# One level of Strassen's scheme in the up-projection of a gated MLP

## The chip, the cores and the metric

The kernel runs on one core of a Trainium2 chip, in one launch. The metric is device time in microseconds of that core; several runs give a median.

## The reference, cut to what matters

One hybrid decoder layer is computed in float32 for a prompt of 2048 tokens and for 8 single-token samples: a first mixing stage (causal pooling and differential attention), cross-attention into 256 memory tokens, and a gated MLP with a causal convolution of width 3 between its two projections. The change touches the MLP:

```python
D_MODEL, D_FF, CONV_W = 1024, 2816, 3

def conv_ffn(h, prefix, w_up, conv_w, conv_b, w_down):
    T = h.shape[1]
    up = h @ w_up                      # (T, 1024) @ (1024, 5632)
    upp = jnp.concatenate([prefix.astype(up.dtype), up], axis=1)
    c = conv_b
    for j in range(CONV_W):
        c = c + upp[:, j:j + T] * conv_w[j]
    a, g = c[..., :D_FF], c[..., D_FF:]
    return (jax.nn.silu(g) * a) @ w_down, upp[:, -(CONV_W - 1):]
```

## The kernel before

**Precision.** Every float32 operand of a large product is split into a rounded high part and a low part, both in the matmul format fp32r (`split`: ScalarE writes the high part, VectorE the difference). A product is three matmuls: low weight by high input, high by high, high weight by low input.

**Layout.** Activations lie transposed, features on the 128 partitions and tokens along the row, in four chunks `c` of 512 tokens; the last also has the 8 samples, `W = [512, 512, 512, 520]`. Its matmuls go in two pieces of 260 columns.

**Buffers.** Pool `hp` (function `H`) has 43 buffers of 4 KB a partition for weights, activations and intermediate tiles. Pool `rp` (opened by `raw_open` after the attention) has two more for raw weights, `sp` (`St`) six small ones. PSUM has two tiles of two banks (`PA`) and four of one bank (`PB`).

**Order of work.** The program is a list of items. An item names the weights that it needs, a function that issues its instructions, and a cost; `weave` mixes two lists by these costs, and `drive` (line 396) walks the list. Ahead of an item it stages coming weights in three steps (`Weight.stage`): the transfer on SyncE's queue, the high part on ScalarE, the low part on VectorE. `look(4, 3, 2)` says how many weights ahead each step is. `later` puts work off by some microseconds of cost, `due` calls it. The tile framework then orders the instructions of each engine and adds the waits; each engine and each queue takes its instructions in that order.

**The MLP.** `ffn_items(c)` (line 1649) goes through the 22 blocks `j` of 128 hidden features, in groups of two. For a block `ffn_up` (line 1471) projects the block of `a` (s = 0) and that of the gate (s = 1). Each is one weight of 1024 x 128 and 24 matmuls of 512 columns (`proj`, lines 429 and 432), a tile `up` in PSUM. ScalarE copies the tile to `Uf` (line 1477) and starts the convolution in `cc` (line 1478), VectorE adds two taps (lines 1484, 1485); the gate, the product and the split into `act` come later. After a group of two blocks `ffn_down` (line 1507) multiplies their `act` with two weights of 128 x 1024: for each of 8 output tiles, 6 matmuls into one PSUM bank (line 1524), and VectorE adds the tile to the residual `xf` (line 1531, for pieces of 260 line 1529).

**Around it.** `norm_steps` scales the input of the MLP and splits it into `h3hi` and `h3lo`, the operands `X[c]` (lines 261 to 267). The cross-attention of the samples (`sc_items` for queries and scores, `sc_items2` for values and output) is woven into chunk 0 of the MLP, norms and the final norm of the neighbouring chunks into chunks 1 to 3. Ahead of the MLP stand the input projections (`p1_items`), the pooling, the attention (`att_items`) and the cross-attention of the prompt.

## Time and profile before

| | us |
|---|---|
| median of 3 runs | 3143.33 (3138.91 to 3145.14) |
| the profiled execution, its own time | 3144.37 |
| its span | 3142.6 |
| TensorE matmuls busy | 3016.3 (96%) |
| TensorE weight loads busy | 2609.5 (83%) |
| VectorE busy | 2023.8 (64%) |
| ScalarE busy | 1369.2 (44%) |
| GpSimd busy | 439.5 (14%) |

The mean granted TensorE clock is 0.983 of full speed. Busy times overlap; a matmul's busy time runs on while the next has started, so the pace of a row of matmuls is read from one start to the next or from the chain of waits, not from the mean duration of one. The chain that ended last lies on TensorE for 60% of the span, up-projection 31% and down-projection 14%.

### The profile page before, as it was taken

What the parts mean: (1) busy time and instruction counts of PE and PEld (TensorE: products, weight loads), DVE (VectorE), ACT (ScalarE), POOL (GpSimd) and SP (SyncE); (2) the same over time, 40 slices, a digit from 0 to 9 for tenths busy, and PEclk for the clock granted to TensorE, in tenths of its full rate; (3) what the DMA queues carried; (4) which work ended last, traced back from release to release, by engine and by line L of the source; (5) the groups of instructions that cost most, each with busy time, mean ns of one, the idle gap of its engine ahead of it and who ended that gap; (6) DMA issues with size and microseconds to landing.
All of it is one profiled execution on the core that took longest, in us unless ns stands there. A gap on an engine that the chain in (4) does not pass through costs nothing.

```text
span 3142.6 us, 45471 instructions
## 1 busy us (share of the span) xinstructions
PE 3016.3 (96%) x17694; PEld 2609.5 (83%) x17694; DVE 2023.8 (64%) x3280; ACT 1369.2 (44%) x2187; POOL 439.5 (14%) x873
## 2 busy tenths in 40 slices
PE   7999999898999989999899999999999999999998
PEld 6889899787897886799777777888888878899998
DVE  5725654568677686645578777766766666766566
ACT  5524444456655423333344444434444433443342
POOL 0134234211111153300000000000000100000000
PEclk9999999999999999999999999999999999999999
DMA  8556356543533385463465334342333433243321
GB/s 285 180 160 218 101 169 187 147 131 120 157 100 109 141 268 195 140 215 132 159 236 180 127 122 151 120 154 91 94 104 118 162 95 112 88 142 96 94 81 71
DMA packets 378203, 451.98 MB, mean 144 GB/s; under 512 B 18321, under 2 KB 292248, under 8 KB 377972
## 3 DMA queue, kind: packets, MB, share of 16 engines
q1 hardware_dynamic: 336925, 349.29, 34.7%
q0 software_dynamic: 27264, 89.03, 8.2%
q10 hardware_dynamic: 13798, 10.76, 1.1%
q8 instruction: 139, 2.28, 0.3%
q14 instruction: 77, 0.62, 0.1%
HBM read 364.57 MB, written 84.85 MB: 143 GB/s over the span
## 4 chain that ended last, share of the span: by engine, by line
PE 60%; DVE 4%; DMA 2%; issue 1%; ACT 1%; POOL 1%; SPq 0%; DVEq 0%; ACTq 0%; POOLq 0%
PE up L429 21%; PE down L1524 14%; PE up L432 10%; PE wo L443 4%; PE vo L94 2%; PE vo L95 2%; PE vo L96 2%; PE S L94 1%; PE S L96 1%; PE S L95 1%; DMA vg<-in_cache_v_dram,idx 1%; DVE wlo L297 1%; DMA mixr<-mix_d 1%; PE O L1123 1%; POOL vg L951 1%
## 5 line engine op out<-in xcount | busy, mean ns | idle before, releaser
L429 PE MATMUL up<-h3hi,wlo 128*128 128x512 f32 (+1 forms) x1760 | 562.6, 352 | 7.5 <-DVE wlo L297 6.8
L429 PE MATMUL up<-h3hi,whi 128*128 128x512 f32 (+1 forms) x1760 | 560.2, 351 | 0.0
L297 DVE TENSOR_TENSOR wlo<-wraw,whi 128x1024 fp32r<-128x1024 f32 x432 | 520.4, 1219 | 50.3 <-ACT whi L294 49.6
L294 ACT CAST whi<-wraw 128x1024 fp32r<-128x1024 f32 x432 | 443.2, 1047 | 195.0 <-DMA wraw<-in_w_down_dram 95.9
L1524 PE MATMUL down<-act,whi 128*128 128x512 f32 (+1 forms) x1760 | 447.5, 352 | 10.9 <-DVE xf L1531 10.1
L432 PE MATMUL up<-h3lo,whi 128*128 128x512 f32 (+1 forms) x1760 | 357.7, 349 | 0.0
L429 PEld LDWEIGHTS up<-h3hi,wlo 128*128 128x128 f32 x1760 | 308.6, 189 | 56.8 <-ACT whi L294 3.8
L429 PEld LDWEIGHTS up<-h3hi,whi 128*128 128x128 f32 x1760 | 308.8, 189 | 46.4
L1524 PEld LDWEIGHTS down<-act,whi 128*128 128x128 f32 x1760 | 293.8, 188 | 60.4 <-DVE xf L1531 13.8
L1484 DVE SCALAR_TENSOR_TENSOR cc<-Uf,vec,cc 128x512 f32<-128x512 f32 x176 | 132.0, 750 | 328.5 <-ACT cc L1478 324.0
L1477 ACT COPY Uf<-up 128x512 f32<-128x512 f32 (+1 forms) x176 | 103.3, 587 | 509.9 <-PE up L432 507.0
L432 PEld LDWEIGHTS up<-h3lo,whi 128*128 128x128 f32 x1760 | 285.6, 188 | 46.6
L1524 PE MATMUL down<-act,wlo 128*128 128x512 f32 (+1 forms) x880 | 279.4, 350 | 0.4 <-DVE wlo L297 0.4
L1483 POOL COPY halo<-Uf 128x2 f32<-128x2 f32 x176 | 44.2, 251 | 1388.0 <-ACT Uf L1477 1377.4
L1531 DVE TENSOR_TENSOR xf<-xf,down 128x512 f32<-128x512 f32 (+1 forms) x308 | 205.5, 682 | 44.7 <-PE down L1524 41.1
L1089 ACT ACTIVATE T<-T,mn 128x1024 f32<-128x1024 f32 (+4 forms) x192 | 171.9, 897 | 132.1 <-DVE mn L1082 122.3
L1071 PE MATMUL sc<-K,Q 128*128 128x512 f32 (+5 forms) x640 | 171.2, 385 | 18.7 <-DVE mn L1082 18.4
L1082 DVE CUSTOM_DVE_ANT_0 T<-sc,Dt 128x1024 f32<-128x1024 f32 (+7 forms) x128 | 125.8, 985 | 76.2 <-PE sc L1071 74.5
L1524 PEld LDWEIGHTS down<-act,wlo 128*128 128x128 f32 x880 | 154.0, 188 | 24.8 <-DVE wlo L297 1.2
L443 PE MATMUL z<-h1hi,wlo 128*128 128x512 f32 (+1 forms) x480 | 158.4, 363 | 4.8 <-DVE pps L668 4.4
L443 PE MATMUL z<-h1hi,whi 128*128 128x512 f32 (+1 forms) x480 | 153.9, 353 | 0.0
L1123 PE MATMUL O<-V,wT 128*128 128x128 f32 x1088 | 149.2, 278 | 1.8 <-ACT wT L1114 1.3
(417 smaller groups left out, 5846.5 us busy)
## 6 DMA issues: line engine op xcount, KB each, us to landing
wraw<-in_w_up_dram SPq DMA_DIRECT2D x176, 512.0 KB
wraw<-in_w_down_dram SPq DMA_DIRECT2D x88, 512.0 KB
wraw<-in_w_in_dram SPq DMA_DIRECT2D x32, 512.0 KB
Q<-q_d SPq DMA_DIRECT2D x64, 256.0 KB
wraw<-in_w_out_dram SPq DMA_DIRECT2D x32, 512.0 KB
wraw<-m_d SPq DMA_DIRECT2D x32, 512.0 KB
wraw<-vo_d SPq DMA_DIRECT2D x32, 512.0 KB
K<-k_d SPq DMA_DIRECT2D x24, 512.0 KB
```

The costliest lines, as they stand in the source:

```text
L294: S.copy(self.hi[:, :1024], self.raw[:, :1024])
L297: V.tensor_tensor(self.lo[:, :1024], self.raw[:, :1024], f(self.hi[:, :1024]), ALU.subtract)
L429: PE.matmul(out, w[wi][:, kt, :], kslice(hi, kt, c0, n), start=kt == 0 and wi == 1, stop=False)
L432: PE.matmul(out, w[0][:, kt, :], kslice(lo, kt, c0, n), start=False, stop=kt == KT - 1)
L443: PE.matmul(out, w[wi][:, kt, :], kslice(z, kt, c0, n), start=i == 0, stop=i == 3 * KT - 1)
L1071: PE.matmul(ps[:, j * 512:j * 512 + w], v3(Q[c], 2)[:, z, self.t * P:(self.t + 1) * P], K[c][hf][:, c0:c0 + w], start=z == 0, stop=z == 1)
L1082: V.tensor_tensor_reduce(out, pin, din, -SLOPE[self.h], 3.0e38 if hf == 0 else mn[:, 0:1], ALU.add, ALU.min, mn[:, hf:hf + 1])
L1089: S.activation(tg[:, :mg], tg[:, :mg], AF.Exp, bias=mn[:, last:last + 1], scale=-1.0, accum_out=self.l[:, 2 * g + c:2 * g + c + 1])
L1123: PE.matmul(O[:, self.t * P:(self.t + 1) * P], self.wt[g][:, (j % 4) * P:(j % 4 + 1) * P], v3(Vt[j // 8], 8)[:, j % 8, :], start=j == 0, s ...
L1484: V.scalar_tensor_tensor(cc[:, :CH], U[:, 1:1 + CH], vc(CWT + FT + nt), cc[:, :CH], ALU.mult, ALU.add)
L1524: PE.matmul(out, ws[p][wi][:, nt, :], act[:, z + c0:z + c0 + n], start=st_ and p == 0, stop=en and p == 1)
L1531: V.tensor_tensor(sv(xx, c), sv(xx, c), view, ALU.add)
```

## The change

One level of Strassen's scheme (in the form with 15 additions) is put on the up-projection. For a block `j` the pair of weights, `a` and gate, is taken as a matrix of 2 x 2 parts: the two halves of the 1024 input features by the two outputs. The chunk's tokens are two halves of 256 (260 in the last chunk). Seven products (`p1`, `p6`, `p5`, `p3`, `p2`, `p7`, `p4` in `ffn_up`) of 512 features by 128 outputs by 256 tokens take the place of eight; each is 12 matmuls.

- Four of the seven weights are sums of parts. `sums_items` makes them once per block, in high and low parts, and writes them to a DRAM tensor `s_d`; blocks 0 to 7 beside the projections of the first two chunks, 8 to 21 beside those of the last two and the attention. In the MLP they are read back as they are (`Stored`, tile `shl`). The other three are half-size weights, split as before (`HalfWeight`, tile `whl`, raw data in four buffers of `rp`).
- The seven token operands of a chunk are made by `xop_items`, in high and low parts, from the scaled input, which is no longer split by `norm_steps`.
- VectorE adds the products out of PSUM, seven additions a pair; ScalarE only copies the first. The conv's first step reads the sum in SBUF.
- The down-projection takes groups of four blocks (`GROUPS`, the last has two), so that a PSUM tile sums 12 matmuls of four blocks; its weights come as 512 rows x 256 columns, and its tiles are spread between the products of the next group.
- `NBUF_H` goes from 43 to 41. `look(6, 3, 2)` is set for the MLP. `sc_items2` moves to chunk 1.

The diff, cut:

```diff
+GROUPS = [4] * 5 + [2]
+HW = CX // 2
-NBUF_H = 43
+NBUF_H = 41
+    qp = ctx.enter_context(tc.tile_pool(name="qp", bufs=6))
+    s_d = [dr.tile([P, 2, 2, 2, 512], F32, name=f"s_d{j}") for j in range(NF)]
...
+    class HalfWeight:
+        def stage(self, n):
+            if n == 0:
+                self.raw = rp[0].tile([P, 512], F32, tag="raw", name="wraw2")
+                SY.dma_start(v3(self.raw, 4, P), self.src)
+            elif n == 1:
+                self.hl = H("whl", F32R)
+                S.copy(self.hl[:, :512], self.raw)
+            else:
+                V.tensor_tensor(self.hl[:, 512:1024], self.raw, f(self.hl[:, :512]), ALU.subtract)
...
+    class Stored(HalfWeight):
+        def stage(self, n):
+            if n == 0:
+                self.hl = H("shl", F32R)
+                SY.dma_start(f(v3(self.hl, 2)), self.src)
...
+        def add(j):
+            def fn(_):
+                wa, wg = st[j]
+                a1, a2, g1, g2 = wa[:, :512], wa[:, 512:1024], wg[:, :512], wg[:, 512:1024]
+                V.tensor_tensor(g2, g1, g2, ALU.add)
+                V.tensor_tensor(g1, a1, g1, ALU.subtract)
+                V.tensor_tensor(a1, g2, a1, ALU.subtract)
+                V.tensor_tensor(a2, a2, a1, ALU.subtract)
+            return item([], fn, 0, 2.5)
+        def part(j):
+            def fn(_):
+                for i, t in enumerate(st.pop(j)):
+                    hi, lo = H("shi", F32R), H("slo", F32R)
+                    split(hi[:, :1024], lo[:, :1024], t[:, :1024])
+                    for z, p in enumerate((hi, lo)):
+                        ST.dma_start(s_d[j][:, i, z].rearrange("p s n -> p (s n)"), f(p[:, :1024]))
...
+        def parts(key, src):
+            hi, lo = H("xhi", F32R), H("xlo", F32R)
+            for i in range(2):
+                split(k4(hi)[:, 2 * i:2 * i + 2, :n], k4(lo)[:, 2 * i:2 * i + 2, :n], src[i])
+            out[key] = k4(hi)[:, :, :n], k4(lo)[:, :, :n]
...
+        return [item([], fn, 0, 2.5) for fn in (p1, t1, t2, q2, t3, p2, t4)]
-    def ffn_up(c, j, s):
-            _, view = proj(c, X[c], ws[0], "up")
-            S.copy(sv(U[:, 2:2 + w], c), view)
-            S.activation(sv(cc[:, :w], c), view, AF.Identity, bias=vc(CB + nt), scale=vc(CWT + 2 * FT + nt))
+    def ffn_up(c, j):
+        def product(out, ws, key):
+            (wh, wl), (xh, xl) = ws[0], X[c][key]
+            for k in range(4):
+                for wi in (wl, wh):
+                    PE.matmul(out, wi[:, k, :], xh[:, k], start=k == 0 and wi is wl, stop=False)
+            for k in range(4):
+                PE.matmul(out, wh[:, k, :], xl[:, k], start=False, stop=k == 3)
+        def add(out, bank, key):
+            V.tensor_tensor(out, bank, st[key][:, :n], ALU.add)
...
+        def p1(ws):
+            two("1", "6")
+            product(st["1"], ws, "1p")
+            st["s1"] = Qt("s1")
+            S.copy(st["s1"][:, :n], st["1"])
+        def p6(ws):
+            product(st["6"], ws, "t2")
+            st["s2"] = Qt("s2")
+            add(st["s2"][:, :n], st["6"], "s1")
...
+        def p4(ws):
+            product(st["4"], ws, "t4")
+            add(st["Ug"][:, 2:2 + n], st["4"], "s2")
+            conv(st["Ug"], NF + j, 1)
...
+            S.activation(cc[:, :w], U[:, 2:2 + w], AF.Identity, bias=vc(CB + nt), scale=vc(CWT + 2 * FT + nt))
...
+        return [item([half_w(j * P, 0)], p1, cost), item([stored(0, 0)], p6, cost), item([stored(1, 1)], p5, cost),
+                item([stored(0, 1)], p3, cost), item([half_w(j * P, 1)], p2, cost), item([stored(1, 0)], p7, cost),
+                item([half_w(DFF + j * P, 1)], p4, cost)]
-    def ffn_down(c, j0):
+    def ffn_down(c, j0, g):
-                for p in range(2):
+                for p in range(g):
+            src = a["w_down"][0, j0 * P:(j0 + g) * P, nt * P:(nt + per) * P].rearrange("(j p) n -> p j n", p=P)
+            return lambda: Weight(src, g)
...
+            for i in range(g):
+                u = ffn_up(c, j + i)
+                k = -(-(len(dn) - 2 * last) // min(g - i, 2 + (i == 0)))
+                d, dn = dn[:k], dn[k:]
+                for k, cuts in enumerate((u[:2], u[2:4], u[4:6], u[6:])):
+                    out += cuts + d[k:k + 1]
+            out += xops * last + dn
...
+    main = weave(half[12:24] + [item([], pool_prep)] + half[24:-8], sums_items(range(8)), 0.0, 0.55)
+    order += weave(weave(late[:-10] + att23[0] + late[-10:], att01[1]), sums_items(range(8, NF)), 0.0, 0.9)
...
+    order += [look(6, 3, 2)]
+    order += weave(ffn_items(0, xops[0]), sc_items + n3[1], 0.02, 0.9)
+    order += weave(ffn_items(1, xops[1]), final(0) + sc_items2 + n3[2], 0.2, 0.9)
```

The framework's order of the instructions shows how the work moves; three places.

TensorE, inside the MLP with 512 tokens, before: the end of one projected tile and the start of the next (`up`); the two alternating rows stand sixteen times a tile.

```order
L429 MATMUL up<-h3hi,wlo 128x512
L429 MATMUL up<-h3hi,whi 128x512
L432 MATMUL up<-h3lo,whi 128x512 x8
L429 MATMUL up<-h3hi,wlo 128x512
L429 MATMUL up<-h3hi,whi 128x512
```

The same engine with the change, chunk 1: a down tile (`down`, four blocks) and two products with half-size weights, 8 + 4 matmuls each.

```order
L1728 MATMUL down<-act,whi 128x512 x2
L1728 MATMUL down<-act,wlo 128x512
L1728 MATMUL down<-act,whi 128x512 x2
L1728 MATMUL down<-act,wlo 128x512
L1612 MATMUL up<-xhi,whl 128x256 x8
L1614 MATMUL up<-xlo,whl 128x256 x4
L1612 MATMUL up<-xhi,whl 128x256 x8
L1614 MATMUL up<-xlo,whl 128x256 x4
```

Matmuls of 512 columns are now 256 wide in the up-projection, and down tiles stand between products. Over the program 5280 up matmuls become 7392.

VectorE in the MLP, before: taps (`cc<-Uf`), low parts of whole weights (`wlo`), gate, down sums (`xf`).

```order
L1484 SCALAR_TENSOR_TENSOR cc<-Uf,vec,cc 128x512
L297 TENSOR_TENSOR wlo<-wraw,whi 128x1024
L1485 SCALAR_TENSOR_TENSOR cc<-Uf,vec,cc 128x512
L297 TENSOR_TENSOR wlo<-wraw,whi 128x1024
L1498 TENSOR_TENSOR cc<-cc 128x512
L1531 TENSOR_TENSOR xf<-xf,down 128x512 x3
L90 TENSOR_TENSOR act<-cc,act 128x512
L1531 TENSOR_TENSOR xf<-xf,down 128x512 x3
```

VectorE in the MLP with the change: additions out of PSUM (line 1617, into the intermediate sums `s` or into `Uf`), low parts of half-size weights (`whl`) and of a down weight (`wlo`), down sums, taps.

```order
L1617 TENSOR_TENSOR s_27968<-up,s_27928 128x256
L96 TENSOR_TENSOR act<-cc,act 128x512
L330 TENSOR_TENSOR whl<-wraw_27891,whl 128x512
L311 TENSOR_TENSOR wlo<-wraw,whi 128x1024
L1732 TENSOR_TENSOR xf<-xf,down 128x512
L1617 TENSOR_TENSOR Uf<-up,s_27968 128x256
L330 TENSOR_TENSOR whl<-wraw_27950,whl 128x512
L1732 TENSOR_TENSOR xf<-xf,down 128x512
L330 TENSOR_TENSOR whl<-wraw_27970,whl 128x512
L1617 TENSOR_TENSOR Uf<-upB,s_27910 128x256
L1674 SCALAR_TENSOR_TENSOR cc<-Uf,vec,cc 128x512
L1617 TENSOR_TENSOR Uf<-up,s_27968 128x256
```

Low parts of coming weights now stand behind additions, each of which follows a product on TensorE.

SyncE's queue at the input projections, before: seven weights (`w_in`) in a row.

```order
L291 DMA wraw<-in_w_in_dram 128x8x128 x2
L783 DMA spl<-in_state_pool_dram 120x512
L291 DMA wraw<-in_w_in_dram 128x8x128 x7
L291 DMA wraw<-in_w_in_dram 128x4x256
L552 DMA xt_1959<-in_x_prompt_dram 128x1024
```

The same place with the change, from the weights behind `spl` on (`wa`, `wg`: the two up weights of a block).

```order
L1520 DMA wa<-in_w_up_dram 128x8x128
L1520 DMA wg<-in_w_up_dram 128x8x128
L305 DMA wraw<-in_w_in_dram 128x8x128
L1520 DMA wa<-in_w_up_dram 128x8x128
L1520 DMA wg<-in_w_up_dram 128x8x128
L1520 DMA wa<-in_w_up_dram 128x8x128
L1520 DMA wg<-in_w_up_dram 128x8x128
L305 DMA wraw<-in_w_in_dram 128x8x128
L1520 DMA wa<-in_w_up_dram 128x8x128
L1520 DMA wg<-in_w_up_dram 128x8x128
L305 DMA wraw<-in_w_in_dram 128x8x128 x2
```

The reads for the weight sums stand between the projection weights, two to four of them ahead of a weight.

## Rows read from the trace of the kernel before

**Rows 1.** The page, part 1: busy us, share of the span, instructions.

```profile
PE 3016.3 (96%) x17694; PEld 2609.5 (83%) x17694; DVE 2023.8 (64%) x3280; ACT 1369.2 (44%) x2187; POOL 439.5 (14%) x873
```

**Rows 2.** Stretches, chunks 0 to 3 of the MLP: us; busy by engine; clock; DMA share; GB/s.

```profile
1554.00:1990.00 436.00, 419.18 (x1877) 326.30 (x1877) 323.32 (x428) 195.58 (x260) 17.56 (x92) 0.98 0.48 158
1990.00:2363.00 373.00, 372.63 (x1634) 302.05 (x1633) 249.88 (x339) 156.90 (x211) 20.42 (x92) 1.00 0.36 112
2363.00:2739.00 376.00, 373.99 (x1641) 302.83 (x1640) 250.57 (x343) 157.50 (x212) 24.04 (x97) 1.00 0.36 117
2739.00:3112.00 373.00, 372.71 (x3116) 372.15 (x3116) 234.13 (x427) 143.60 (x195) 18.24 (x91) 1.00 0.31 98
```

**Rows 3.** The chain of waits inside a chunk of 512: start us, us, what.

```profile
2306.68 11.15 PE down L1524 x48
...
2323.38 3.70 PE up L429 x16
2327.08 1.85 PE up L432 x8
```

**Rows 4.** The chain of waits inside chunk 3, pieces of 260.

```profile
2841.59 3.82 PE up L429 x32
2845.41 1.92 PE up L432 x16
...
2858.82 11.42 PE down L1524 x96
```

**Rows 5.** Instructions in order of time, TensorE, scores: first and 45th of 45 matmuls.

```profile
1483.20 0.28 PE L95 MATMUL S<-whi,h2hi 128*128 128x256 f32 x1
...
1488.42 0.28 PE L94 MATMUL S<-wlo,h2hi 128*128 128x256 f32 x1
```

**Rows 6.** The page, part 5: weight loads; busy us, mean ns of one, idle before.

```profile
L429 PEld LDWEIGHTS up<-h3hi,wlo 128*128 128x128 f32 x1760 | 308.6, 189 | 56.8 <-ACT whi L294 3.8
```

**Rows 7.** Groups of instructions by form, VectorE: busy us, mean ns, idle before.

```profile
L297 DVE TENSOR_TENSOR wlo<-wraw,whi 128x1024 fp32r<-128x1024 f32 x432 | 520.4, 1219 | 50.3 <-ACT whi L294 49.6
L1531 DVE TENSOR_TENSOR xf<-xf,down 128x512 f32<-128x512 f32 x264 | 175.2, 681 | 43.5 <-PE down L1524 40.0 <-DMA xf<-x_d 1.1
L1484 DVE SCALAR_TENSOR_TENSOR cc<-Uf,vec,cc 128x512 f32<-128x512 f32 x176 | 132.0, 750 | 328.5 <-ACT cc L1478 324.0 <-ACT ast L89 3.4 <-ACT ost L89 0.7
L90 DVE TENSOR_TENSOR act<-cc,act 128x512 fp32r<-128x512 f32 x66 | 45.4, 687 | 18.6 <-ACT act L89 18.5
L1529 DVE TENSOR_TENSOR xf<-xf,down 128x260 f32<-128x260 f32 x88 | 33.2, 418 | 2.0 <-PE down L1524 1.9
```

**Rows 8.** The same view, VectorE, cross-attention of the samples.

```profile
L90 DVE TENSOR_TENSOR cvl<-cmv,cvh 128x1024 fp32r<-128x1024 f32 x16 | 19.2, 1218 | 0.5 <-ACT cvh L89 0.5
L1372 DVE TENSOR_TENSOR cmk<-cmk,qcb 128x1024 f32<-128x1024 f32 x16 | 19.2, 1216 | 0.0
L1373 DVE TENSOR_REDUCE scs<-cmk 128x4 f32<-128x1024 f32 x16 | 19.2, 1211 | 0.0
...
L1425 DVE COPY sco<-sco 8x512 f32<-8x512 f32 x16 | 10.6, 674 | 14.1 <-PE sco L1422 14.1
```

**Rows 9.** Stretches, as in rows 2: a busy one of chunk 0.

```profile
1600.00:1700.00 100.00, 92.69 (x393) 74.00 (x392) 89.97 (x107) 39.51 (x54) 5.65 (x22) 0.97 0.66 231
```

**Rows 10.** Stretches, as in rows 2: ahead of the MLP.

```profile
10.00:20.00 10.00, 7.19 (x41) 7.19 (x41) 5.42 (x5) 5.24 (x5) 0.00 (x0) 1.00 1.06 393
...
140.00:230.00 90.00, 90.00 (x420) 73.55 (x419) 22.25 (x40) 25.54 (x46) 28.82 (x52) 1.00 0.46 139
...
290.00:500.00 210.00, 202.55 (x1334) 183.81 (x1333) 122.33 (x287) 97.09 (x204) 63.69 (x111) 0.98 0.50 152
...
1400.00:1554.00 154.00, 147.86 (x867) 130.22 (x866) 88.99 (x126) 52.21 (x86) 5.23 (x10) 0.98 0.42 148
```

**Rows 11.** Groups of instructions, GpSimd: one issue of 512 KB.

```profile
L226 POOL DMA_DIRECT2D x_d<-x x16 | 10.5, 658 | 125.3 <-DVE x L1215 101.3 <-DVE x L1307 12.5 <-DMA wraw<-vo_d 11.5
```

**Rows 12.** Waits: engine, line, waited for, us in total, times, longest.

```profile
ACT whi L294 <- DMA wraw<-in_w_down_dram: 95.9, 20, 7.6
```

More of the change, by code (lines that the diff above doesn't have):

```diff
@@ L214, in sv, with sum_squares @@
         return ap if W[c] == CH else ap.rearrange("p (a b) -> p a b", a=2)
+    def sum_squares(xs, w, name):
+        s = None
+        for q in range(4):
+            sq = H(name)
+            S.activation(x3(sq)[:, :, :w], x3(xs[q])[:, :, :w], AF.Square)
+            if q:
+                V.tensor_tensor(x3(s)[:, :, :w], x3(s)[:, :, :w], x3(sq)[:, :, :w], ALU.add)
+            s = s or sq
+        if w > CH:
+            G.memset(sq[:, w:CH + P], 1.0)
+        V.tensor_tensor(sq[:, :w], x3(s)[:, 0, :w], x3(s)[:, 1, :w], ALU.add)
+        return sq
     def norm_steps(c, x, g0, name, done, spill=None, rs=None):
@@ L288, in stage @@
             if n == 0:
[L289 to L290 removed]
+                self.raw = H("wraw")
                 SY.dma_start(v3(self.raw, self.k), self.src)
@@ L1188, in att_items @@
         return first, out
-    X = {}
+    X, xn = {}, {}
     def p3_items(c):
@@ new lines, in k4, with xop_items, block, both_halves @@
+    def k4(t):
+        return t[:, :4 * HW].rearrange("p (k n) -> p k n", k=4)
+    def xop_items(c):
+        n = W[c] // 2
+        st, out = {}, {}
+        X[c] = out
+        def block(half, t):
+            return [x3(xn[c][2 * half + i])[:, :, t * n:(t + 1) * n] for i in range(2)]
+        def both_halves(t):
+            return [k4(t)[:, 2 * i:2 * i + 2, :n] for i in range(2)]
+        def parts(key, src):
[3 more added lines that the diff above has]
+            out[key] = k4(hi)[:, :, :n], k4(lo)[:, :, :n]
+        def sub(dst, x, y):
+            for i in range(2):
+                V.tensor_tensor(dst[i], x[i], y[i], ALU.subtract)
+        def p1(_):
+            parts("1p", block(0, 0))
+        def t1(_):
+            st["t1"] = both_halves(H("t1"))
+            sub(st["t1"], block(0, 1), block(0, 0))
+            parts("t1", st["t1"])
+        def t2(_):
+            st["t2"] = both_halves(H("t2"))
+            sub(st["t2"], block(1, 1), st["t1"])
+            parts("t2", st["t2"])
+        def q2(_):
+            parts("2q", block(1, 1))
+        def t3(_):
+            sub(block(0, 1), block(1, 1), block(0, 1))
+            parts("t3", block(0, 1))
+        def p2(_):
+            parts("2p", block(1, 0))
+        def t4(_):
+            sub(block(1, 0), block(1, 0), st["t2"])
+            parts("t4", block(1, 0))
+        return [item([], fn, 0, 2.5) for fn in (p1, t1, t2, q2, t3, p2, t4)]
```

192 lines of the change are left out of this document (109 added, 83 removed).

## The prediction

> **What bounds the kernel now.** I read the page first, then a table by stretches, then the chain of waits inside two stretches, then single rows. The page shows TensorE busy 96% of the span and VectorE 64% [rows 1]. Cut at the four chunks of the feed-forward stage, which fills 1554 to 3112 us, half the span, TensorE is busy 419 of 436 us in the first chunk and all but 0.3 to 2 us in the others, at a granted clock of 1.00 (the 2.4 GHz level); VectorE works 63 to 74% [rows 2]. The chain inside chunk 2 runs over matmuls alone: 24 matmuls of 512 columns, one projected tile, take 3.70 + 1.85 = 5.56 us (232 ns each), and 48 of the down-projection 11.15 us [rows 3]. In chunk 3 (520 tokens as two pieces of 260) a tile is 48 matmuls in 3.82 + 1.92 = 5.74 us, 119.6 ns each [rows 4]. So this stage is TensorE's, and every column taken out of it is time, as long as VectorE follows.
>
> **Up-projection on TensorE.** Before: 132 tiles x 5.56 + 44 tiles x 5.74 = 986.5 us. After: seven products of 12 matmuls for a pair of tiles, half the tokens wide. Rows of 256 columns stand in the scores: 44 start-to-start steps between 1483.20 and 1488.42, 118.6 ns each, with another weight at most steps [rows 5]. So 66 pairs x 84 x 118.6 ns = 657.5 us, and 22 pairs x 84 x 119.6 ns = 221.0 us, 878.5 in all: **108 us less**. (Seven eighths would be 123; the rest goes because a matmul of 256 columns costs 51% of one of 512.) What could contradict this is the weight load, 189 ns each [rows 6] and one per matmul; at 118.6 ns a step two of them overlap, and did in rows 5. The Trainium skill, "TensorE: Matmul & The Clock Gate", section "Back-to-back issue gap", speaks against the change: a stream of load and matmul pairs is said to settle near 81 ns at 128 columns and 131 ns at 512, so halving the columns would not halve the time. Estimated from that page, 3168 matmuls of 512 (415 us) would become 5544 of 256 at some 98 ns (543 us), 128 us worse; the steps in rows 3 and 5 (232 and 118.6 ns) disagree with it. The down-projection keeps its matmuls: 0.
>
> **VectorE in the feed-forward.** Per pair of tiles it did, from [rows 7]: two low halves of up weights 2 x 1.22, one of a down weight 1.22, four conv taps 4 x 0.75, gate and low half of the activation 2 x 0.69, four down sums 4 x 0.68: 10.8 us, against 2 x 5.56 + 5.58 = 16.7 us of TensorE (64%; rows 2 have 67% with the norms). It will do: three half-size low halves 3 x 0.69, the down weight 1.22, the same taps and gate, two down sums (four tiles are now summed in PSUM) 1.36, and seven additions of a product out of PSUM; the nearest row is the 260-wide down sum, 0.42 us each, 2.9. Together 11.9 us against 9.96 + 5.58 = 15.5 of TensorE: 77%. Per chunk come 14 low halves and 8 differences of the token operands, 22 x 0.69 = 15 us (4.9 before), square sums and scalings of one or two norms (each 8 x 0.75 + 3 x 1.22 + 0.69 = 10.4), and the sample group: in chunk 0 its scores (16 products and 16 reductions of 1.22, eight weight splits, 49 us), and in chunk 1, where the change moves them, its values (16 x 1.22 + 16 x 0.67 + 8 x 1.22 = 40 us) [rows 8]. Sums, VectorE against TensorE (220 of products, 111 to 137 of down, the rest the sample group and transposes): chunk 0 332 of 339, chunk 1 339 of 375, chunk 2 299 of 348, chunk 3 287 of 362. VectorE never needs more than TensorE, but in the first two chunks it needs nearly as much.
>
> What that costs I take from the stretch where it was so before: at 1600 to 1700 VectorE was 90% busy and TensorE 92.7%, granted 0.97 [rows 9]. The engine takes its queue in order, and the change queues the low half of a coming weight behind additions that wait for a product, so a late product holds up the next weight. Losses over TensorE's own time: chunk 0 8% of 339 = 27 (about 30 now: 17 idle in rows 2, the rest matmuls that ran slower than in rows 3); chunk 1 6% = 22 (1 now); chunk 2 3% = 10 (3 now); chunk 3 2% = 7 (1 now). The differences are **+31 us**, between -30 and 120. One wait is moved: the conv's first step on ScalarE now follows VectorE's second addition and not the product itself, with weight roundings queued behind it; its result is needed a group of four pairs later, 60 us, so 0, and without that cover it would join the losses above.
>
> **Chunk borders.** The operands of the next chunk (15 us of VectorE) are made while TensorE has only two down tiles, 2 x 2.79 us; its first product needs only the first operand, the second the third one. About 2 us at each of three borders: **+6**, 0 to 20. For chunk 0 they lie beside the cross-attention, 1400 to 1554, where VectorE was 58% busy [rows 10]: 0; without that cover 15.
>
> **Weight sums.** 22 blocks, each four additions of 0.69, two low halves of 1.22 (5.2 us of VectorE), two roundings on ScalarE, whose share stays under half, four writes of 512 KB from GpSimd and two reads. The first eight go behind the projections at 115 to 195 us, 14 into the attention at 290 to 500. There VectorE was at 25% (140 to 230) and 58% [rows 10]; with 42 and 73 us more it fits in both, at 93% in the second. Transfers: 8 x 3.15 MB in some 80 us and 14 x 3.15 MB in 210 come to about 310 and 210 GB/s, on top of 139 and 152; the most a stretch of 10 us moved was 393 [rows 10]. So the first batch asks for more than was ever seen, and SyncE's queue, in order, has projection weights behind these reads: 8 us; the second batch costs like rows 9, 7% less a cover in the matmuls of the late projections, 12. **+20**, 0 to 70. GpSimd gets 88 issues of 0.66 us [rows 11], 58 us in stretches where it was 30% busy: 0, and with no cover it would delay only writes nobody waits for at once. "DMA: Bandwidth & Descriptors", section "Specifications", of the Trainium skill puts a core's share of HBM at about 358 GB/s. By that figure the first batch would need (12 + 25 MB) / 358 = 105 us in a stretch of 80 to 90, some 20 us late instead of 8, and the sum would be -39; a 10 us stretch at 393 in rows 10 lies above that figure.
>
> ScalarE loses 176 copies out of PSUM and gains less: 0. Weight traffic in the stage rises from 1.57 to 3.4 MB a pair, some 245 GB/s with the rest against 112; a share of 0.36 becomes about 0.8, which rows 10 and the page's first slices (285 GB/s) bear: 0 in the sum, and rival 3 if they do not. SyncE issues 8 transfers a pair instead of 3, each behind the one before, and two of the large buffers are given up; both count there too.
>
> **Sum:** -108 + 31 + 6 + 20 = -51. The profiled execution took 3144.4 us (span 3142.6), 1 us above the median of the runs shown, 3143.3. Forecast: **3093 us**, its own range 3050 to 3130.
>
> **Rivals.** (1) *VectorE's queue sets the pace, and the kernel is slower.* There are 264 half-size weights. If the addition (0.42) and the low half behind it (0.69) stood uncovered before each product, that would be 290 us. It decides from 0.34 us per half weight on (108 - 20 = 88 us over 264); at 0.45 us it is 119, and 3144 - 108 + 20 + 6 + 119 = 3181. For it: the demand of 98% in chunk 0, and that a low half is made two weights ahead, now 2.4 to 5 us of matmuls, where it was 11. Against: four of seven products take ready operands from DRAM and need no VectorE. Chance 0.18. (2) *Nothing is lost.* PSUM slack covers the additions, the sums fit, and the 30 us that chunk 0 loses now go with the moved sample values: 3144 - 108 - 30 = 3006, with part of the losses 3040. VectorE's demand speaks against it. 0.15. (3) *The transfers take the gain back*, by weights that land late; ScalarE already waited 96 us on down weights in 20 waits at a DMA share near 0.4 [rows 12]: with 100 us of such waits reaching TensorE, 3140. 0.07. (4) *Matmuls go by weight loads.* If loads did not overlap, 7392 x 189 ns = 1397 us, 3144 - 986 + 1397 = 3555. It is the mechanism behind the skill's section named above, in a sharper form; rows 5 exclude it nearly. 0.02. That the products are not made at half size is no rival: the order of matmuls shows 7392 of 256 or 260 columns for 5280.
>
> **How the numbers follow.** The forecast has 0.58. Faster by over 0.2% (6 us, what a measurement can tell here): 0.58 + 0.15 = 0.73; within: 0.07; slower: 0.18 + 0.02 = 0.20. The range 3035 to 3165 holds the forecast and rival 3, a third of rival 2 and a third of rival 1: 0.76 to 0.8; left out are the rest of rivals 1 and 2 and all of 4.
>
> **What would show it.** Up matmuls of 256 columns at 117 to 120 ns from start to start, the stage 1554 to 3112 some 70 us shorter; VectorE above 90% busy in chunks 0 and 1, and TensorE's idle time there ended by VectorE (low halves, additions) or by ScalarE behind it; little idle time ended by transfers; up to 20 us lost before 550. Wrong: steps over 125 ns, idle time of TensorE in the stage over 120 us or ended by transfers, or a loss before 550 above 40 us.

## The result and the profile after

The changed kernel takes 3167.11 us (median of 4 runs, 3163.08 to 3169.07) against 3144.23 us for the kernel before in the same session (4 runs, 3138.91 to 3147.94): a ratio of 1.0072, 95% interval [1.0054, 1.0091]. It is slower by 0.7%; the forecast was 3093 us, faster by 1.6%. The profiled execution took 3165.4 us, its span is 3163.7 us, and its page reads, against [rows 1]:

```profile
PE 2958.2 (94%) x19806; PEld 2662.8 (84%) x19806; DVE 2244.5 (71%) x4032; ACT 1350.8 (43%) x2271; POOL 506.9 (16%) x961
```

The first question is where the 21 us between the spans lie. The view of the tile `up` gives the first and last start of the products of the MLP (behind the count: the shortest, median and longest duration in ns):

```profile
L1612 PE MATMUL up<-xhi,whl x1408: 274/281/507, 1643.6 to 3127.1; 128*128 128x256 f32 x132, 128*128 128x260 f32 x44
```

The MLP starts at 1643.6 us; before it started at 1554.1. So **89.5 us are lost ahead of the MLP**, and the MLP with the rest of the program takes 3163.7 - 1643.6 = 1520.1 us where it took 1588.5: **68.4 us are won inside it**. The two halves are read apart.

**Inside the MLP.** Stretches from the first product of a chunk to that of the next, the last one up to the last product; columns as in [rows 2]:

```profile
1643.60:2003.00 359.40, 350.20 (x2413) 318.73 (x2412) 293.19 (x488) 144.05 (x227) 17.96 (x91) 0.99 0.79 265
2003.00:2397.50 394.50, 383.84 (x2629) 340.57 (x2628) 317.39 (x558) 167.63 (x250) 26.45 (x92) 1.00 0.72 240
2397.50:2762.70 365.20, 356.60 (x2432) 326.28 (x2431) 280.76 (x498) 142.48 (x222) 26.84 (x97) 0.99 0.71 231
2762.70:3127.60 364.90, 358.89 (x2873) 350.57 (x2871) 273.79 (x581) 133.65 (x206) 26.50 (x92) 0.99 0.64 212
```

The forecast had 366, 397, 358 and 369 us and 2 us a border; the stretches are 359, 395, 365 and 365. VectorE is busy for 82, 80, 77 and 75% of them, TensorE idles for 6 to 11 us in each, and transfers move 212 to 265 GB/s. What TensorE waited for in the whole of it (us in total, times, longest):

```profile
engine line waited for: us in total, times, longest us
PE down L1728 <- ACT whi L308: 8.4, 4, 3.8
PE down L1728 <- DVE wlo L311: 7.5, 7, 1.5
PE up L1612 <- DVE s L1617: 3.6, 6, 1.0
...
PE up L1612 <- DMA shl<-s_d: 1.1, 1, 1.1
```

ScalarE and VectorE end most of these waits, and stored sums that come late cost 1.1 us in one wait. The pace of products stands in the order of time, TensorE, chunk 0 (start, us):

```profile
1900.79 1.11 PE L1612 MATMUL up<-xhi,shl 128*128 128x256 f32 x8
1901.73 0.64 PE L1614 MATMUL up<-xlo,shl 128*128 128x256 f32 x4
1902.21 1.10 PE L1728 MATMUL down<-act,whi 128*128 128x512 f32 x3
```

Twelve matmuls of 256 columns go from 1900.79 to 1902.21, 118.3 ns each.

**Ahead of the MLP.** The stretches of [rows 10], and the one from the first scores of the attention to its output projection, first with the change, then before:

```profile
290.00:500.00 210.00, 182.12 (x1170) 163.01 (x1169) 144.23 (x294) 96.63 (x182) 70.74 (x114) 0.95 0.75 240
140.00:230.00 90.00, 78.70 (x330) 62.71 (x329) 52.95 (x75) 34.86 (x50) 33.91 (x65) 0.94 0.99 351
310.00:690.00 380.00, 316.57 (x2057) 282.76 (x2058) 237.63 (x496) 171.24 (x332) 133.13 (x215) 0.92 0.77 248
```

```profile
310.00:610.00 300.00, 284.62 (x1966) 260.26 (x1965) 160.12 (x378) 136.03 (x282) 91.67 (x147) 0.97 0.51 155
```

Behind the first projections (140 to 230) the transfer engines are busy nearly all the time, a share of 0.99. In the attention VectorE is at 63% (238 of 380 us), far from full, and yet TensorE fell from 95% busy to 83%, and its mean granted clock from 0.97 to 0.92. At the lower of the clock's two levels, 1.2 GHz, twelve matmuls of 512 columns took 5.49 us (from 382 to 387 the granted clock is 0.50), at the higher, 2.4 GHz, 2.78 us (1.00 from 446.3 to 449); start, us, what, from the chain of waits:

```profile
381.99 5.49 PE z L484 x12
446.53 2.78 PE z L484 x12
```

If the mean clock is one over time, 16% of the 380 us, 61 us, went at the lower level. So an estimate of what the clock costs in this stretch is up to 30 us, against up to 9 in the 300 us before. The chain of waits from 300 to 700 (shares by line, then start, us, what) names a culprit at once:

```profile
by line: DMA wg<-in_w_up_dram 21.0%; PE z L484 12.0%; issue 10.8%; PE sc L1112 5.9%; PE O L1164 4.8%; DMA s_d<-shi 4.2%; DMA wraw<-in_w_out_dram 3.3%; DVE T L1123 2.8%; PE v L102 2.3%; DVE Wn L693 2.3%; PE v L100 2.3%; PE v L101 2.3%; PE wT
...
312.52 9.34 DMA wg<-in_w_up_dram
414.43 10.34 DMA wg<-in_w_up_dram
...
499.16 12.11 DMA wg<-in_w_up_dram
```

A fifth of it, 84 us, is the landing of `wg`, the second raw weight of a block of sums. VectorE's queue in order of time shows what that does:

```profile
418.53 0.48 DVE L1147 SCALAR_TENSOR_TENSOR T<-T,rc 128x256 f32<-128x256 f32 x1
424.79 0.69 DVE L1528 TENSOR_TENSOR wg<-wg 128x512 f32<-128x512 f32 x1 [5.78 <-DMA wg<-in_w_up_dram]
425.40 0.70 DVE L729 SCALAR_TENSOR_TENSOR ql<-z,qh 128x520 fp32r<-128x520 f32 x1
426.01 0.68 DVE L1529 TENSOR_TENSOR wg<-wa,wg 128x512 f32<-128x512 f32 x1
426.61 0.16 DVE L733 TENSOR_TENSOR zsT<-qh,ql 128x8 f32<-128x8 f32 x1
426.69 0.68 DVE L1123 CUSTOM_DVE_ANT_0 T<-sc,Dt 128x512 f32<-128x512 f32 x1
```

The first addition of a block (line 1528) stands 5.8 us at the head of the queue, and the row maximum of the attention (line 1123) comes only behind it. The totals from 240 to 700, VectorE's and TensorE's, and TensorE's in the kernel before, 240 to 610:

```profile
DVE wg L1528 <- DMA wg<-in_w_up_dram: 52.4, 11, 9.1
```

```profile
PE sc L1112 <- DVE mn L1123: 34.3, 12, 13.3
```

```profile
PE sc L1071 <- DVE mn L1082: 6.9, 7, 2.6
```

TensorE's waits for row maxima grow from 6.9 to 34.3 us.

### The profile page after: what moved, and what is told of

Its sections match the earlier page's. It is cut to its first block, busy times and chain, and to the rows that moved or that the text cites. A ratio compares the mean times of both kernels' runs of the same rounds, so it can differ in the third digit from the quotient of the medians.

```text
span 3163.7 us, 52554 instructions
## 1 busy us (share of the span) xinstructions
PE 2958.2 (94%) x19806; PEld 2662.8 (84%) x19806; DVE 2244.5 (71%) x4032; ACT 1350.8 (43%) x2271; POOL 506.9 (16%) x961
## 4 chain that ended last, share of the span: by engine, by line
PE 69%; DVE 9%; DMA 7%; issue 6%; ACT 2%; POOL 1%; SPq 0%; DVEq 0%; ACTq 0%; POOLq 0%
PE up L1612 14%; PE down L1728 14%; PE up L1614 7%; PE wo L484 4%; PE O L1164 3%; PE z L484 3%; PE sc L1112 3%; DMA wg<-in_w_up_dram 3%; PE upB L1612 2%; PE S L100 2%; PE S L102 2%; PE S L101 2%; PE vo L100 2%; PE vo L101 2%; PE vo L102 2%
## 5 line engine op out<-in xcount | busy, mean ns | idle before, releaser
L1612 PE MATMUL up<-xhi,shl 128*128 128x256 f32 (+1 forms) x2816 | 406.7, 286 | 5.1 <-ACT s L1627 1.8
L1612 PEld LDWEIGHTS up<-xhi,shl 128*128 128x128 f32 x2816 | 369.5, 189 | 37.1 <-ACT s L1627 11.2
L1666 ACT ACTIVATE cc<-Uf,vec 128x512 f32<-128x512 f32 (+1 forms) x176 | 144.0, 818 | 528.4 <-DVE Uf L1617 520.8
L311 DVE TENSOR_TENSOR wlo<-wraw,whi 128x1024 fp32r<-128x1024 f32 x256 | 308.6, 1218 | 38.8 <-ACT whi L308 26.4
L308 ACT CAST whi<-wraw 128x1024 fp32r<-128x1024 f32 x256 | 265.0, 1047 | 131.8 <-DMA wraw<-in_w_down_dram 30.0
L1671 POOL COPY halo<-Uf 128x2 f32<-128x2 f32 x176 | 59.2, 336 | 1312.9 <-DVE Uf L1617 1273.1
L1614 PE MATMUL up<-xlo,shl 128*128 128x256 f32 (+1 forms) x1408 | 225.1, 282 | 0.0
L1612 PE MATMUL up<-xhi,whl 128*128 128x256 f32 (+1 forms) x1408 | 200.1, 285 | 5.1 <-DVE whl L330 3.0
L1612 PEld LDWEIGHTS up<-xhi,whl 128*128 128x128 f32 x1408 | 184.3, 190 | 13.9 <-DVE whl L330 5.2
L1614 PEld LDWEIGHTS up<-xlo,shl 128*128 128x128 f32 x1408 | 192.2, 189 | 0.2
L330 DVE TENSOR_TENSOR whl<-wraw,whl 128x512 fp32r<-128x512 f32 x264 | 178.9, 684 | 0.2
```

The source lines that it names most:

```text
L308: S.copy(self.hi[:, :1024], self.raw[:, :1024])
L311: V.tensor_tensor(self.lo[:, :1024], self.raw[:, :1024], f(self.hi[:, :1024]), ALU.subtract)
L330: V.tensor_tensor(self.hl[:, 512:1024], self.raw, f(self.hl[:, :512]), ALU.subtract)
L1612: PE.matmul(out, wi[:, k, :], xh[:, k], start=k == 0 and wi is wl, stop=False)
L1614: PE.matmul(out, wh[:, k, :], xl[:, k], start=False, stop=k == 3)
L1666: S.activation(cc[:, :w], U[:, 2:2 + w], AF.Identity, bias=vc(CB + nt), scale=vc(CWT + 2 * FT + nt))
```

## The experiments

Two numbers are read from each trace: when the MLP starts, and how long it is from the first scores matmul (`sc`) to there, which leaves the first batch of sums (blocks 0 to 7, ahead of the scores) out. With the change the scores start at 308.4, so the second is 1335.2 us; before, 292.8 and 1261.3. Four theories of the second batch (blocks 8 to 21): W, the wait at the head of VectorE's queue; D, the demand of its own work; T, its transfers; B, the large buffers. Most kernels of this section ran once; single runs of the kernel before lay between 3137.9 and 3150.2, so a difference of 5 us is not read, and one of 8 or 10 is weak.

**Is it the sums at all?** All but one block are left out.

```diff
-sums_items(range(8)), 0.0, 0.55)
+sums_items(range(1)), 0.0, 0.55)
-weave(weave(late[:-10] + att23[0] + late[-10:], att01[1]), sums_items(range(8, NF)), 0.0, 0.9)
+weave(late[:-10] + att23[0] + late[-10:], att01[1])
-Stored(s_d[j][:, i, :, s, :])
+Stored(s_d[0][:, i, :, s, :])
```

> Left out: the weight sums of 21 of the 22 blocks; the MLP reads the stored sums of block 0 for every block, with the same transfers. The first up-projection matmul starts at 1554 us before and at 1644 with the change, so 90 us are lost ahead of the MLP and 68 won inside it. If the sums cost all of the 90: the MLP starts at 1555 to 1565 and the time is 3167 - 85 = 3082 (3075 to 3095), whatever the mechanism. If part of the loss comes from something else that the change brings (41 buffers instead of 43, the new norm code): the MLP starts later than 1580 and the time stays above 3100.

Measured: 3090.1 us, in the first range, with an MLP start between the two that were named. Its MLP took 1519.9 us, as with all sums.

```profile
L1612 PE MATMUL up<-xhi,whl x1408: 274/281/468, 1568.5 to 3052.1; 128*128 128x256 f32 x132, 128*128 128x260 f32 x44
```

The scores start at 295.4 instead of 308.4, so the first batch (but for the one block that stays) costs 13; from there to the MLP it is 1273.1 instead of 1335.2, so the second costs 62. But the MLP starts at 1568.5 and not at 1554: 14 us belong to something else.

**Two buffers fewer**, in the kernel before (`NBUF_H = 43` to 41):

> The kernel before with 41 large buffers instead of 43, and nothing else. With one block of sums the MLP still starts at 1568.5 instead of 1554, 14 us late, of which 12 are lost in the attention (295 to 625). Theory B (two buffers fewer make the weights and the softmax tiles late): 3150 to 3158, first scores matmul to first output projection 325 to 332 us instead of 317.5. Otherwise (the new norm code, scatter): 3136 to 3146.

Measured: 3155.3 us, and

```profile
L429 PE MATMUL up<-h3hi,wlo x1760: 277/391/632, 1567.3 to 3108.5; 128*128 128x512 f32 x118, 128*128 128x260 f32 x78
```

The MLP starts 13 us later, and 11 of them are lost between the first scores and the last (755 us against 744); from there to the MLP the two kernels are alike, 517 and 518 us. So nearly all of the 14 us are the two buffers, which the change gave up for its six small ones. The prediction had them at 0. In time the cost is smaller: beside this run the kernel before took 3148.5 us, 6.8 less, so 13, read against the trace of another session, may be some us too much.

**The second batch in pieces.** Without its reads, additions from one resident block; then with the reads back, into buffers that nobody reads; then with neither reads nor writes; then reads and writes alone.

```diff
 # no reads (block 7's weights stay resident), new outputs
-wa, wg = st[j]
+wa, wg = st[js[0] - 1]; na, ng = H("na"), H("ng")
 # reads unused: as above, and
+out += [load(j + 1)]
 # compute only: no reads, and
-ST.dma_start(s_d[j]..., f(p[:, :1024]))
 # transfers only: no additions and no split
-split(hi[:, :1024], lo[:, :1024], t[:, :1024])
+ST.dma_start(s_d[j]..., t[:, :1024])
```

> Left out: the DRAM reads of the second batch of sums (blocks 8 to 21); its additions take one resident block instead and write to other buffers, with the same count of additions, splits and writes. Theory W (the first addition of a block stands at the head of VectorE's queue until the block's raw gate weight has landed, 52 us in 11 waits between 240 and 700, and row maxima of the attention are queued behind it): the MLP starts 50 to 60 us earlier, near 1590, time 3105 to 3115. Theory D (the 5.2 us of VectorE and 2.1 us of ScalarE a block are what collides): nothing changes, 3155 to 3170. Theory T (the 3.15 MB of transfers a block delay the attention's own loads): a third of them is gone, 3135 to 3145.

> As the kernel without the second batch's reads, but with these reads put back at their old places, into buffers that no engine reads; the additions still take one resident block (so the sums of blocks 8 to 21 are not those of the weights). All transfers, additions and splits are there, only VectorE's wait for a landing is not. Theory W: still 3105 to 3120. Theory T: back to 3150 to 3170, and the waits show the attention's weights and Q, K, V late. Theory D: 3155 to 3170.

> Left out: reads and writes of the second batch; additions, roundings and low parts stay in place (the MLP reads the stored sums of blocks 0 to 7 for all). The kernel without reads starts its MLP at 1618, that with one block at 1568.5: 50 us, of which some 14 are the first batch (it moves the first scores matmul from 295 to 311). Theory D (VectorE's and ScalarE's own work collides): those 36 us stay, 3132 to 3140. Theory T (512 KB writes that queue behind the attention's own transfers, and buffers held until they land): 3100 to 3112.

> Left out: the additions, roundings and low parts of the second batch; its reads and writes stay (each raw weight is written twice), with two buffers a block instead of six. Theory D: only what the reads cost is left, 20 us over the kernel with one block plus its first batch: 3115 to 3128. Theory T: 3135 to 3155.

| second batch | time | MLP starts | scores to MLP | over none |
|---|---|---|---|---|
| none | 3090.1 | 1568.5 | 1273.1 | |
| compute only | 3122.4 | 1599.4 | 1290.4 | 17 |
| transfers only | 3123.3 | 1598.3 | 1289.0 | 16 |
| no reads | 3139.0 | 1617.8 | 1306.5 | 33 |
| reads unused | 3159.1 | 1638.5 | 1327.1 | 54 |
| the change | 3167.1 | 1643.6 | 1335.2 | 62 |

Neither work nor transfers alone cost more than 17 us, though each alone brings nearly all of its load into the stretch: VectorE goes from 181 to 234 us, the transfers from 144 to 280 GB/s. Columns as in [rows 2], none, compute only and transfers only:

```profile
309.00:647.00 338.00, 320.23 (x2142) 291.17 (x2141) 181.20 (x420) 150.58 (x311) 98.30 (x157) 0.95 0.47 144
```

```profile
309.00:647.00 338.00, 306.61 (x2075) 277.76 (x2074) 233.81 (x497) 173.32 (x336) 103.04 (x159) 0.96 0.50 152
```

```profile
309.00:647.00 338.00, 308.47 (x2073) 278.94 (x2072) 175.09 (x415) 148.45 (x309) 130.27 (x217) 0.95 0.84 280
```

Together they cost 62. No theory fits all four runs: without reads the time is in T's range, transfers only in D's, compute only in neither. But the edits change the buffers too. Transfers only holds two large buffers a block instead of six, and the other three runs keep block 7's two buffers through the whole batch; the next group of runs asks what that is worth. W, which the chain had made so plain, falls here as a price of 50 to 60 us: with the reads unused, VectorE's wait for landings went from 52 us to 11 (an output that took the buffer of an unread load), and 8 us came back. How much more it would have been with block 7's buffers free is not shown. TensorE's waits in that run, 300 to 690, show what else was late:

```profile
PE sc L1112 <- DVE mn L1123: 20.8, 11, 10.3
PE sc L1112 <- DMA Q<-q_d: 20.5, 5, 7.6
```

The row maxima still are late, and the attention's own queries are late now too, 20.5 us where they were 2.5 with the change. It seems that one wait had covered the other.

**Buffers and queues.** The second batch stays where it is; with 43 large buffers (the three intermediate sums of a pair in one of them); then the low half written over the sum, four buffers a block instead of six; then, in the unaltered change, its writes from ScalarE's queue, and its reads from GpSimd's.

```diff
-NBUF_H = 41
+NBUF_H = 43
-st["s1"] = Qt("s1")
+q = H("s"); st["s1"] = q[:, :HW]
 # in place
-hi, lo = H("shi", F32R), H("slo", F32R)
+hi, lo = H("shi", F32R), t.bitcast(F32R)
 # writes from ScalarE
-ST.dma_start(s_d[j]...)
+(S if js[0] else ST).dma_start(s_d[j]...)
 # reads from GpSimd
-SY.dma_start(v3(t, 8), a["w_up"]...)
+(ST if js[0] else SY).dma_start(v3(t, 8), a["w_up"]...)
```

> The change with its sums where they were, but 43 large buffers (the intermediate sums of a pair share one large buffer). Alone, the second batch's work put the MLP back by 15 us and its transfers by 14, with both but no reads it was 34, with everything 60: more than the sum. Theory B (a block holds six buffers until its writes have landed, and SyncE's queue, in order, waits for a free one ahead of every later load): two buffers more give back more here than the 13 us that they are worth without sums: MLP at 1610 to 1622, time 3130 to 3142. Theory D+T (work and transfers collide wherever buffers are): 13 us and no more, MLP near 1630, 3150 to 3156.

> As the run with 43 buffers, and the low half of a sum is written over the sum itself: a block holds four large buffers instead of six, everything else as it was. Theory B: another 15 to 25 us, 3108 to 3125. Theory D+T: no change, within 5 us of that run.

> The change as it is (41 buffers, six a block, same place), but the DRAM writes of the second batch are issued from ScalarE's queue instead of GpSimd's. If buffers are held because the writes stand in GpSimd's queue behind softmax steps: the MLP starts 15 to 35 us earlier than at 1643.6, time 3130 to 3150. If only the count of buffers matters: within 6 us of 3165. If ScalarE's own queue suffers (it would wait for the low half on VectorE ahead of its exponentials): 3170 to 3200.

> The change as it is (41 buffers, six a block, same place), but the second batch's reads of raw weights are issued from GpSimd's queue. If the reads, waiting in SyncE's queue for a free buffer, hold back the attention's own weights and Q, K, V behind them: the MLP starts 20 to 40 us earlier than at 1643.6, time 3125 to 3147. If it is the buffers or the collision of work and transfers whatever the queue: 3158 to 3172. If GpSimd, which takes a step in every softmax row, is blocked instead: 3175 to 3200.

Measured, time and scores to MLP: 43 buffers 3153.9 and 1322.2; in place as well 3136.5 and 1302.2; writes from ScalarE 3162.5 and 1329.4; reads from GpSimd 3162.8 and 1331.6. Two buffers give 13 us back, hardly more than the 11 that they are worth without sums, as D and T had it. Two buffers fewer a block give another 20, where D and T had none and B 15 to 25. So neither stands alone. Over the kernel before, which has 43 buffers too (1261.3), the second batch costs 61 us with six buffers a block and 41 with four, with the same work and the same transfers: of the 29 us by which 62 exceeds 17 + 16, some 20 go with the buffers of a block, and what is left is weak. That work and transfers make each other dearer is therefore shown only for a batch that holds six buffers a block. Why four a block help, and two more in the pool give no more than they do without sums, is not settled. The queues of the writes and of the reads are out, each within 6 us. With the writes on ScalarE's queue VectorE's wait for `wg` fell by 31 us, from 52.4, and 6 us came back, another case in which the length of that wait is not its price (300 to 690):

```profile
DVE wg L1528 <- DMA wg<-in_w_up_dram: 21.2, 7, 4.5
```

**Another place.** The second batch goes to the end of the cross-attention, where GpSimd is nearly idle and TensorE goes through long rows of matmuls; with 41 and 43 buffers; spread over three and four places; over a longer end.

```diff
-order += sc_[2][8:] + wo[3]
-order += weave(vo[2], n2[3], 0.0, 0.9) + weave(sc_[3] + vo[3], n3[0] + xop_items(0), 0.4, 1.0)
+end = sc_[2][8:] + wo[3]
+end += weave(vo[2], n2[3], 0.0, 0.9) + weave(sc_[3] + vo[3], n3[0] + xop_items(0), 0.4, 1.0)
+order += weave(end, sums_items(range(8, NF)), 0.0, 0.95)
```

> The second batch is moved whole, waits and all, from the attention (290 to 650) into the last part of the cross-attention (some 250 us ahead of the MLP), where VectorE was 50 to 58% busy and GpSimd idle before. Theory W: the wait for the raw weights comes along, but less is queued behind it that TensorE needs at once: 3100 to 3125. Theory D: VectorE goes to 85%: 3085 to 3100. Theory T: 165 + 176 = 340 GB/s are asked for there: 3130 to 3160.

> The kernel with the second batch late in the cross-attention (3131.7), with 43 large buffers again: the three intermediate sums of a pair go into one large buffer and the pool of small ones is dropped. Theory B: the 12 to 14 us ahead of the MLP come back, 3115 to 3122, if the MLP does as well with some two buffers fewer for weights. Otherwise 3128 to 3136.

> 43 buffers, low halves in place, and the sums spread: 5 blocks beside the first projections, 8 in the second half of the attention, 9 late in the cross-attention. The kernel with 8 first and 14 late loses 12 us in the first place and 16 late (3113). Theory B: thinner and with fewer buffers, the loss falls to 10 to 18 in all: 3095 to 3106. Theory D+T: the second half of the attention, where VectorE is 71% busy, costs as much as the first did: 3113 to 3125.

> The same with four places: 4 blocks first, 5 beside the late projections, 6 in the second half of the attention, 7 late. If thin is what counts: 3092 to 3104. If the late projections are bad at any density (4 us a block, as in the change): 3110 to 3120.

> As c4, but only 5 blocks in the first place and 17 over the last two fifths of the cross-attention (about 1250 to 1580). If the first place costs 1.5 us a block and the late one 1: 3095 to 3108. If the added stretch, where VectorE and the transfers were busiest before (86%, 0.75), collides: 3112 to 3130.

Measured, time and scores to MLP: late 3131.7 and 1295.1; with 43 buffers 3113.0 and 1276.8; three places 3136.7 and 1298.3; four 3130.7 and 1295.3; the longer end 3112.8 and 1280.3. The place is worth 40 us of the 62, although VectorE's share before was 58% in both [rows 10]. The late run lies in T's range. Two more buffers give 18 us there. The runs in three and in four places lie above every range that was named for them: thin is not what counts. Eight blocks in the second half of the attention cost 24 us (first output projection to last scores 629.2 to 1081.8, against 622.1 to 1051.2 without them), 14 at the end with 43 buffers 16. Why the place counts is argued and not shown: both the long rows of TensorE and the idle GpSimd set it apart.

**The best version, and the wait again.** Late, low halves in place, with 43 buffers; with 42 and four small ones; and the latter with the second batch's reads on GpSimd's queue. Each of these three ran four times.

```diff
-NBUF_H = 41
+NBUF_H = 42
-qp = ctx.enter_context(tc.tile_pool(name="qp", bufs=6))
+qp = ctx.enter_context(tc.tile_pool(name="qp", bufs=4))
```

> The second batch late in the cross-attention, 43 large buffers, low halves of the sums written in place (four buffers a block). With six buffers a block this place cost 16 us for 14 blocks. If buffers limit it there too: 3098 to 3108. If it is the 330 GB/s asked for in that stretch, or VectorE: 3110 to 3118. Against the kernel before a ratio of 0.985 to 0.991.

> As the run before it, but 42 large buffers and a pool of four small ones for the intermediate sums. The MLP took 1520 us with 41 and small ones, 1525 to 1529 with 43 shared: 5 us come back there, and up to 6 are lost ahead of it. Within 5 us of the run before it.

> The best version so far (3100, 42 buffers and four small ones, low halves in place, second batch late) with the second batch's reads on GpSimd's queue, which is idle there. If SyncE's queue costs something late too: 3090 to 3097. Otherwise 3097 to 3106.

Measured: 3106.5 us, a ratio of 0.9875 [0.9855, 0.9895]; 3100.1 us, **0.9863 [0.9835, 0.9892]**; and 3124.0 us, 0.9931 [0.9909, 0.9952]. The second beats both kernels (the first of the three, 6 us above it, is not told apart from it): its MLP takes 1522.5 us, and from scores to MLP it is 1266.5 us, 5 more than before. Late, the low halves in place give only 4 us (1273.0 against 1276.8). The third missed its expectation, which had it equal or better, and became a control. GpSimd takes a read only behind the writes that stand ahead of it in its queue, and from 1380 to 1600 these writes waited 49.3 us for low halves in `wa`, against 20.6 in the best version. The work and the bytes, 683 MB, are the same; VectorE's wait from 1380 to 1600 and two stretches, first of the best version, then with the reads on GpSimd:

```profile
DVE wg L1528 <- DMA wg<-in_w_up_dram: 2.8, 1, 2.8
```

```profile
1380.00:1480.00 100.00, 95.37 (x606) 85.77 (x605) 75.30 (x104) 34.04 (x41) 17.84 (x33) 0.98 1.01 370
1480.00:1580.00 100.00, 89.83 (x559) 80.48 (x558) 88.49 (x127) 49.79 (x88) 14.98 (x29) 0.95 0.88 309
```

```profile
DVE wg L1528 <- DMA wg<-in_w_up_dram: 25.6, 6, 9.3
```

```profile
1380.00:1480.00 100.00, 87.50 (x511) 77.16 (x511) 65.22 (x91) 31.87 (x38) 27.16 (x42) 0.91 0.92 336
1480.00:1580.00 100.00, 82.44 (x555) 75.81 (x554) 78.68 (x110) 45.98 (x79) 23.99 (x38) 0.90 0.84 302
```

The wait for `wg` grows by 22.8 us, and the MLP starts 25.3 us later:

```profile
L1612 PE MATMUL up<-xhi,whl x1408: 274/281/415, 1574.2 to 3060.2; 128*128 128x256 f32 x132, 128*128 128x260 f32 x44
```

```profile
L1612 PE MATMUL up<-xhi,whl x1408: 274/281/415, 1599.5 to 3086.1; 128*128 128x256 f32 x132, 128*128 128x260 f32 x44
```

The medians are 23.9 us apart. So here the wait costs about its own length, and in neither run did TensorE wait for a transfer of its own in that stretch; in the attention, where queries and row maxima were late too, 41 us less of it gave 8 us.

## Why the prediction was wrong

**The up-projection, -108: right.** Products go at 118 ns a matmul, with a new weight at each, as the scores did [rows 5]. The rule of the Trainium skill, "TensorE: Matmul & The Clock Gate", section "Back-to-back issue gap", by which the halving would not have paid (81 ns at 128 columns, 131 at 512), disagrees with this trace: 512 columns take 232 ns against its 131, and 256, for which it has no figure, take 118. Rival 4 is out with that.

**VectorE in the feed-forward, +31, and borders, +6: right in sum.** The MLP got 68.4 us shorter, 71 were forecast. Its four stretches took 60 us more than TensorE's own time in the sum (1484 against 1424), where 66 were forecast; TensorE idled for 34 of these, and where the rest went is not shown. A half-weight low half takes 684 ns, an addition 422, a down sum 684 (groups by form, VectorE, in the MLP):

```profile
L330 DVE TENSOR_TENSOR whl<-wraw,whl 128x512 fp32r<-128x512 f32 x261 | 176.9, 684 | 0.2
...
L1732 DVE TENSOR_TENSOR xf<-xf,down 128x512 f32<-128x512 f32 x144 | 98.4, 684 | 36.7 <-PE down L1728 35.2
L1617 DVE TENSOR_TENSOR Uf<-up,s 128x256 f32<-128x256 f32 x198 | 83.5, 422 | 74.1 <-PE up L1614 72.3
```

VectorE is less full than forecast, 82 and 80% in the first two chunks and not above 90; the sign named for that was wrong. The loss came out all the same, which is luck in part, as its rate was taken from a stretch where VectorE was 90% busy. One reason for the smaller share stands in the rows of VectorE's queue above: operations that last 0.68 to 0.70 us start 0.61 apart (424.79, 425.40, 426.01), so durations add up to more than the time that they take. Rival 1 would have needed a fuller VectorE and is out, although its time, 3181, lies nearer to the result than the forecast: the slow kernel it described is not this one. Rival 2, nothing lost, is out by these 60 us and by the sums. Rival 3 is out for the MLP: it needed 100 us of waits, TensorE idled for 34, and stored sums made 1.1 of them at 212 to 265 GB/s.

**Weight sums, +20 (0 to 70): the step that failed.** It was sized for the second batch as "7% less a cover in the matmuls of the late projections, 12", from a stretch of the MLP [rows 9]. It measured 62, and both batches together 75. The step added VectorE's shares, 58% and 73 us, found room, and took its price from a place where TensorE goes through long rows of matmuls. What the runs show in its place: the same batch at the end of the cross-attention, with the same share of VectorE before, costs 40 us less, and in the attention 20 us go away when a block holds four buffers instead of six. A mechanism that fits is that in the attention TensorE's next matmul waits for a maximum on VectorE and an exponential on ScalarE over and over (TensorE waited 34.3 us for maxima and 6.9 before; ScalarE 75 us in 34 waits between 240 and 700, and 49 in 33 before), so that the cover there is not the idle share but the few us that TensorE has in hand. This is argued from the waits; no run isolates it. The step also looked at the transfers and at the work one at a time. Each alone costs 16 or 17 us, which is near the 12; what both do together, with the buffers that they hold until the writes have landed, was not in the sum. How the 62 divide between these causes stays open. The prediction's own rule, to name what is queued behind an added wait, was applied to the conv and not to the additions of the sums.

The first batch, 8, measured 13. By the 358 GB/s of the Trainium skill's "DMA: Bandwidth & Descriptors", section "Specifications", the prediction had estimated 20; the stretch 140 to 230 moved 351 GB/s at a share of 0.99, near that figure. It is no ceiling, though: the best version moved 370 GB/s for 100 us. The Trainium skill's "HBM Reference", section "Specifications (TRN2)", says that a core streaming alone goes well above the share of 358 GB/s; the 370 lie above it, by 3%.

**Two buffers fewer, 0: wrong by up to 13.** The prediction counted them with the transfers and named no cover, and the waits of SyncE's queue for a free buffer were not looked at.

So ahead of the MLP 13 (buffers), 1 that nothing here explains, 13 (first batch) and 62 (second batch) make the 89.5 us, against 20. The sign that was named for it, a loss above 40 us before 550, is there: the last input projection starts at 563.1 instead of 504.5. The range of the term, to 70, was nearly wide enough for its 75; the range of the forecast, 3050 to 3130, took only a part of it, and the wider one, to 3165, ended 2 us short.

## What to carry to other kernels

Side work that is woven into another stage is not priced by that stage's idle shares. Ask at each engine what stands at the head of its queue while an operand is on its way, and what the stage's critical engine needs from behind it; then try the work in another place, first where the critical engine has long rows of its own. Count the buffers that the side work holds until its writes have landed. Here the place gave 40 us, and with the buffers besides a loss of 0.7% became a gain of 1.4%. And a wait that the chain names need not be a price, as something else may be late behind it: take it away in one run before building on it, and see that the edit leaves the buffers as they were.

## What the runs showed of the hardware that was not expected

Work and transfers that cost 17 and 16 us alone cost 62 together, in the same stretch, with VectorE at 63% and the transfers at a share of 0.77; with four buffers a block and 43 in all they cost 41, so part of that is the price of buffers. One core moved 370 GB/s over 100 us, at a share of 1.01.

A stall often goes with a lower clock: in the attention of the changed kernel TensorE idled 63 of 380 us, and its granted clock was 0.92 over the stretch, against 15 of 300 us and 0.97 before; in the control with late reads it was 0.91 and 0.90 where the best version had 0.98 and 0.95. The two do not go in step, though: with compute only TensorE idled 31 of 338 us at 0.96, with one block of sums 18 at 0.95.
